# A two-block network: the residual summed on GpSimd and transposed in two parts, the gate weights in one block

## Chip, core and metric

The kernel runs on one core of a Trainium2 chip. The time is the device time of one execution in microseconds (us); three runs are given for the kernel before. TensorE multiplies, VectorE and ScalarE work element by element and read TensorE's results from the banks of PSUM, GpSimd works on SBUF alone, and SyncE (SP) issues the transfers.

## What is computed

512 tokens of 1024 channels go through two blocks. The first is a sliding-window attention beside a gated convolution, and a feed-forward network. The second takes its normalised output `x`, projects it, and mixes it in three ways: a sparse attention with three gated branches, a stick-breaking attention, a gated recurrence. It ends in an output product, a residual and a layer norm. What the change touches is in the second block:

```
h = x @ w_in                                   # among it 18 columns nsa_g
gates = sigmoid(nsa_g)                         # 6 heads x 3 branches
...
mixed = concat(o_nsa * silu(nsa_z), o_sb * silu(sb_z), o_hg * silu(hg_z))
x = layer_norm(ALPHA * x + mixed @ w_out, ln_g, ln_b)
```

and, in the first block, the mask of the sliding window, a constant "band" of 128 x 256.

## The kernel before

Precision is kept by splitting: a weight or an activation `w` becomes a high part `wh` (ScalarE rounds it to fp32r) and a low part `wl = w - wh` (VectorE), and a product is three matmuls: high x high, high x low, low x high. Activations are kept channel-major, 128 channels by 512 tokens; the second block's input is eight pairs `x2[k] = (h, l)` of such tiles.

`dense` (L218) makes one block of 128 output channels: 8 groups of input channels times three matmuls of 512 tokens into one bank. `Weights` loads the blocks ahead through two `raw` tiles, and `split_w` (L189) splits them. `in_proj2` (L800) calls `dense` for each entry of `ORDER`; the fifth, "ng", is the block of the 18 gate columns (L802 gives it 18 output rows), which `gates2` (L728) turns into `gate`: scale, clamp, four small transposes into one bank, Exp, and 1/(1+e). The last eight entries, "z", are the gates of the outputs.

Beside `in_proj2` run the sparse attention (`sparse`, whose `compress`, L857, adds positions to the compressed keys and values on VectorE), the recurrence and `sticks` (the stick-breaking pairs). In `sticks` a pair of heads makes logits, takes a softplus, cuts it to the strict triangle with GpSimd's `affine_select` (L1008; tiles `dk` and `hk`), sums it with the matmuls `pga<-hk,trir`, exponentiates on ScalarE, cuts again (`lv` and `hk`), and multiplies by the values into `poa`. `SEQ` puts the last such pair at the end of that stream.

A planner drives these four tasks by paced costs; the tile framework then orders each engine's instructions by priority and puts in the waits. An engine works strictly in its own order. Banks have five names: "m", "ga", "gb" (two each), "oa", "ob" (one each). A tile or bank that is asked for anew waits until the readers of the one before are done.

At the end stand the output product and the residual. `load_out` (L1239) loads and splits the two halves of `w_out_2`. The residual must be token-major, so all eight `x2` pairs are transposed by plain matmuls against an fp32r identity (`trir[:, 2]`), high and low part into one bank, 64 in all; ScalarE copies the eight banks out, scaled by the token's norm (`rcol`), as `x2t`. Then comes the first half of the product: for each of 8 `mixed` tiles and 4 groups of 128 tokens three matmuls, 96 in all, into four banks. `add` sums product and residual and takes the statistics. The second half goes token group by token group, each with its layer norm and its store.

Of the kernel before, what the change touches and what calls it, by code (L numbers as in the profile page):

```python
# [18 lines left out]
P = 128  # L19
T = 512  # L20
# [19 lines left out]
_off = 0  # L40
for _n, _w in (
    ("ident", 128), ("bones", 128), ("ntri", 128), ("m8", 128),
    ("band", 256), ("valid", 1),
):
    CM[_n] = (_off, _w)
    _off += _w
# [20 lines left out]
def tile_net(ctx, tc, a, out):  # L67
# [114 lines left out]
        return wp.tile([P, 8, P], F32, tag="raw", name=nm("raw"), bufs=2)  # L182

    def fetch(src, nk, w=P):
        raw = raw_tile()[:, :nk, :w]
        nc.sync.dma_start(raw, src)
        return raw

    def split_w(raw, cuts=(0, 8)):  # L189
        nk, w = raw.shape[1], raw.shape[2]  # L190
        wh = wp.tile([P, 8, P], F32R, tag="wh", name=nm("wh"), bufs=2)[:, :nk, :w]
        wl = wp.tile([P, 8, P], F32R, tag="wl", name=nm("wl"), bufs=2)[:, :nk, :w]
        with tc.high_priority(offset=100):
            for c0, c1 in zip(cuts, cuts[1:]):
                c = slice(c0, min(c1, nk))
                A.copy(wh[:, c], raw[:, c])  # L196
                tt(wl[:, c], raw[:, c], wh[:, c].bitcast(F32), ALU.subtract)
        return wh, wl
# [19 lines left out]
    def dense(ws, xs, use, pre=None, tag="m", rows=P, hold=None):  # L218

        ps = bank(tag)[:rows]  # L220
        k, c = 0, 0
        while k < len(xs):
            wh, wl = ws.take()
            for n in range(wh.shape[1]):
                xh, xl = xs[k]
                mm(ps, wh[:, n], xh, k == 0, False)
                mm(ps, wh[:, n], xl, False, False)
                mm(ps, wl[:, n], xh, False, k == len(xs) - 1)
                k += 1
                c += 1  # L230
                if c == 2:
                    c = 0
                    yield 1.3
        if hold is not None and pre is None:
            hold.append((use, ps))
        else:
            if pre:
                pre()
            for u, p in hold or ():
                u(p)  # L240
            use(ps)
        yield 0.65 * c
# [73 lines left out]
    W1.ahead(3, 0)  # L316
    cst = cp.tile([P, CMW], F32, tag="cst", name="cst")
    nc.sync.dma_start(cst, a["const"])

    def S(n, i=0, w=None):  # L320
        o, full = SM[n]
# [135 lines left out]
    def softmax_a(j, ip):  # L457

        ss = [bank(t) for t in ("ga", "gb")]
        lo = [P if ip == 0 and u == 0 else 0 for u in range(2)]  # L460
        for u in range(2):
            i = 2 * ip + u
            for hh in range(2):
                scores(ss[hh][:, u * 256 + lo[u]:u * 256 + 256], qT[j], kv1["k"], hh,
                       slice(i * P, (i + 1) * P), slice((i - 1) * P + lo[u], (i + 1) * P))
        st = small(20)
        sbs = [wk(), wk()]
        for hh in range(2):
            sk = S("sink", j + 4 * hh, 1)
            for u in range(2):  # L470
                c = slice(u * 256 + lo[u], u * 256 + 256)
                n = 2 * hh + u
                V.tensor_tensor_reduce(
                    sbs[hh][:, c], ss[hh][:, c], C("band")[:, lo[u]:], 1.0, sk, ALU.add, ALU.max, st[:, n:n + 1]
                )
        V.tensor_scalar(st[:, 4:8], st[:, 0:4], -1.0, None, ALU.mult)
        for n in range(4):
            hh, u = divmod(n, 2)
            c = slice(u * 256 + lo[u], u * 256 + 256)
            A.activation(sbs[hh][:, c], sbs[hh][:, c], AF.Exp, bias=st[:, 4 + n:5 + n], accum_out=st[:, 8 + n:9 + n])  # L480
        for hh in range(2):
            A.activation(
                st[:, 12 + 2 * hh:14 + 2 * hh], st[:, 4 + 2 * hh:6 + 2 * hh], AF.Exp, bias=S("sink", j + 4 * hh, 1)
            )
        tt(st[:, 8:12], st[:, 8:12], st[:, 12:16], ALU.add)
        V.reciprocal(st[:, 16:20], st[:, 8:12])
        for n in range(4):
            hh, u = divmod(n, 2)
            c = slice(u * 256 + lo[u], u * 256 + 256)
            V.tensor_scalar(sbs[hh][:, c], sbs[hh][:, c], st[:, 16 + n:17 + n], None, ALU.mult)  # L490
        return sbs, lo
# [234 lines left out]
    gate = cp.tile([P, 4, 18], F32, tag="gate", name="gate")  # L726

    def gates2(ps):  # L728
        t = dk()[0:18]
        stt(t, ps, -1.0, rstd3[0:18], ALU.mult, ALU.mult)  # L730
        V.tensor_scalar(t, t, 80.0, None, ALU.min)
        gps = bank("gb")
        for i in range(4):
            TE.transpose(gps[:, 18 * i:18 * i + 18], t[:, i * P:(i + 1) * P], ident[0:18, 0:18])
        A.activation(gate.rearrange("p i h -> p (i h)"), gps[:, 0:72], AF.Exp)
        V.tensor_scalar(gate, gate, 1.0, None, ALU.add)
        V.reciprocal(gate, gate)

        g0 = gate[:, 0].rearrange("p (h b) -> p h b", b=3)[:, :, 0]
        V.tensor_scalar(g0, g0, C("valid"), None, ALU.mult)  # L740
# [59 lines left out]
    def in_proj2():  # L800
        for n, key in enumerate(ORDER):
            yield from dense(W2, x2, use2(key), norm3 if n == 0 else None,  # L802
                             "m" if n > 3 else alt(n), 18 if key == "ng" else P)
            if n == 4:
                token_scale()
        done.add("proj")
# [432 lines left out]
    def load_out(half):  # L1239
        for n, k in enumerate(KORD):  # L1240
            rv = raw_tile()[:, 0:4].rearrange("p a b -> p (a b)")
            nc.sync.dma_start(rv, a["w_out_2"][half, k])
            wo[half, k] = split(rv, None, of("np") if half == 0 else xt if n < 6 else of("hk"))

    load_out(0)


    x2t = [[None] * 2 for _ in range(4)]
    for half in range(2):
        ps = [bank(t) for t in (("ga", "ga", "oa", "ob"), ("m", "m", "gb", "gb"))[half]]  # L1250
        for k in range(4):
            h, l = x2[4 * half + k]
            for i in range(4):
                mm(ps[i][:, k * P:(k + 1) * P], h[:, i * P:(i + 1) * P], trir[:, 2], True, False)
                mm(ps[i][:, k * P:(k + 1) * P], l[:, i * P:(i + 1) * P], trir[:, 2], False, True)
        for i in range(4):
            x2t[i][half] = nk()
            with tc.high_priority(offset=100):
                A.activation(x2t[i][half], ps[i], AF.Copy, scale=rcol[:, i:i + 1])

    load_out(1)
    lng, lnb = (raw_tile().rearrange("p a b -> p (a b)") for _ in range(2))
    nc.sync.dma_start(lng, a["ln_g"].to_broadcast([P, D]))
# [11 lines left out]
    def add(ps, half, i, c=slice(0, T)):  # L1275
# [2 lines left out]
        V.bn_stats(bns[i][:, seen[i]:seen[i] + 6], y)  # L1278
        seen[i] += 6

    po = [bank(t) for t in ("ga", "ga", "oa", "ob")]
    for n in range(KT):
        for i in range(4):
            product(po[i], n, 0, i)
    for i in range(4):
        add(po[i], 0, i)
    for i in range(4):
        for c, t in ((slice(0, T), alt(i)),) if i < 3 else ((slice(0, 256), "ob"), (slice(256, T), "gb")):
            ps = bank(t)[:, 0:c.stop - c.start]
            for n in range(KT):  # L1290
                product(ps, n, 1, i, c)
            add(ps, 1, i, c)
        ag = small(8)
        V.bn_aggr(ag[:, 0:2], bns[i][:, 0:seen[i]])
        A.activation(ag[:, 3:4], ag[:, 1:2], AF.Ln, bias=eps)
        A.activation(ag[:, 3:4], ag[:, 3:4], AF.Exp, scale=-0.5)
        V.tensor_scalar(ag[:, 2:3], ag[:, 1:2], 1e-5 / (ALPHA * ALPHA), None, ALU.add)
        stt(ag[:, 4:5], ag[:, 3:4], ag[:, 2:3], ag[:, 3:4], ALU.mult, ALU.mult)
        V.tensor_scalar(ag[:, 4:5], ag[:, 4:5], -0.5, 1.5, ALU.mult, ALU.add)
        tt(ag[:, 3:4], ag[:, 3:4], ag[:, 4:5], ALU.mult)  # L1300
        for hf in range(2):
            y = x2t[i][hf]
            stt(y, y, ag[:, 0:1], lng[:, T * hf:T * hf + T], ALU.subtract, ALU.mult)
            stt(y, y, ag[:, 3:4], lnb[:, T * hf:T * hf + T], ALU.mult, ALU.add)
            nc.sync.dma_start(out[i * P:(i + 1) * P, T * hf:T * hf + T], y)
# [9 lines left out]
def _constants():  # L1315
# [7 lines left out]
    c["m8"] = (lt & (p[:, None] // 8 != p[None, :] // 8)).astype(f)  # L1323
    k = np.arange(256)
    band = (k[None] > p[:, None]) & (k[None] <= p[:, None] + P)
    c["band"] = np.where(band, 0.0, NEG).astype(f)
    c["valid"] = (p >= 31).astype(f)[:, None]
    const = np.concatenate([c[n] for n in CM], axis=1)
    ms = []
# [7 lines left out]
    oh[b[ok], np.nonzero(ok)[0]] += 1.0  # L1337
    oh[31, ok] -= 1.0
    oh[32, ~ok] = 1.0
    return np.ascontiguousarray(const), cmi, oh  # L1340


def _cols(v):
# [8 lines left out]
def _layout(i):  # L1352
# [6 lines left out]
    for j in range(8):  # L1359
# [12 lines left out]
    rmix = np.concatenate([q2, r(384, 1024)])  # L1372
    f = np.float32
    w_in, w_in2 = i["w_in"][0], i["w_in_2"][0]
    const, cmi, oh = _constants()
    pos = i["cmp_pos_2"][0].reshape(16, 2, 64).transpose(2, 1, 0).reshape(64, 32)
    small = {
        "mix": _cols(i["mix_norm"][0]), "ffn": _cols(i["ffn_norm"][0]), "fin": _cols(i["final_norm"]),
# [10 lines left out]
    return {  # L1389
        "xT": i["x"][0].T.reshape(KT, P, T),  # L1390
        "small": np.concatenate([small[n] for n in SM], axis=1),
        "const": const, "cmask": cmi, "onehot": oh,
        "tbl": np.concatenate([i["rel_bias_2"], np.full((1, 6), NEG, f)], axis=0),
        "w_in": _blocks(w_in[:, cin]),
        "w_br": br,
# [27 lines left out]
```

## Time and profile before

| what | value |
|---|---|
| time, three runs | 1069.88, 1070.99, 1071.37 us (median 1070.99) |
| profiled execution | 1068.53 us, span 1066.8 us |
| TensorE busy | 1039.5 us, 97% of the span, 5712 matmuls |
| VectorE, ScalarE, GpSimd busy | 704.4 (66%), 488.8 (46%), 44.0 us (4%) |
| granted TensorE clock | 0.999 (mean) |
| chain that ended last | TensorE 75%, VectorE 11%, ScalarE 7%, DMA 3% |

The page gives busy times, the chain of waits that ended last, and groups of instructions. Other views of the same execution give busy times by stretch, and the instructions of an engine in order of time. A row there has the start and the length in us, the engine, the line of the kernel, what is written and read, and, in brackets, how long the engine stood idle before it and what ended that. Rows of equal instructions that follow each other are merged ("x4"), and the length is then that of all of them. Matmuls overlap: a start minus the start before is the time that one takes from TensorE, not its length.

### The profile page before, as it was taken

Reading aid. Unit: us, or ns where it says so; the run is one execution under the profiler, and the core shown is the slowest. Engines: PE = TensorE matmul, PEld = TensorE weight load, DVE = VectorE, ACT = ScalarE, POOL = GpSimd, SP = SyncE. Lnnn points to the kernel's source line nnn. Section 1 sums busy time; section 2 is a strip of 40 time slices with the busy share of each in tenths; the row PEclk is TensorE's granted clock in tenths of the full one; section 3 lists DMA queues with packets and bytes.
Section 4 is the critical chain, followed back from the end, with each engine's and each line's share of the span. In section 5 each row is a group of like instructions: output and inputs, shape, how many; then the busy total and the mean of one; then the engine's idle time right before and its main releaser. Section 6 shows DMA issues by size and latency. Waiting matters only on the chain.

```text
span 1066.8 us, 14636 instructions
## 1 busy us (share of the span) xinstructions
PE 1039.5 (97%) x5712; PEld 838.9 (79%) x5712; DVE 704.4 (66%) x1313; ACT 488.8 (46%) x855; POOL 44.0 (4%) x89
## 2 busy tenths in 40 slices
PE   8999999999999999999999999999999999989997
PEld 6788888888888888888877888767777777767886
DVE  6876643356448777777763233597967698887757
ACT  5754443322344444444442222433625676578740
POOL 0000000000220000000000111200000000011000
PEclk9999999999999999999999999999999999999999
DMA  6212232333432233223335333531321110101232
GB/s 218 79 60 80 79 94 85 99 99 109 142 120 85 98 99 99 98 99 99 99 94 193 97 106 90 184 101 41 99 75 47 59 41 22 41 21 37 82 120 79
DMA packets 32801, 97.84 MB, mean 92 GB/s; under 512 B 4878, under 2 KB 5390, under 8 KB 32732
## 3 DMA queue, kind: packets, MB, share of 16 engines
q1 hardware_dynamic: 32732, 96.91, 28.7%
q8 instruction: 45, 0.74, 0.3%
q14 instruction: 24, 0.20, 0.1%
HBM read 94.77 MB, written 5.27 MB: 94 GB/s over the span
## 4 chain that ended last, share of the span: by engine, by line
PE 75%; DVE 11%; ACT 7%; DMA 3%; issue 2%; SPq 1%; POOL 1%; DVEq 0%; POOLq 0%; ACTq 0%
PE pm L139 44%; PE pob L139 12%; PE poa L139 12%; PE pga L139 4%; PE pgb L139 3%; DVE wl L136 2%; DMA raw<-in_w_in 1%; ACT wh L196 1%; DVE lv L136 1%; DMA raw<-in_w_down 1%; DVE hk L136 1%; DVE dk L136 1%; DVE np L136 1%; DVE nk L942 1%; ACT nk L948 1%
## 5 line engine op out<-in xcount | busy, mean ns | idle before, releaser
L139 PE MATMUL pm<-x,wh 128*128 128x512 f32 (+1 forms) x1360 | 433.4, 395 | 2.1 <-DVE x L133 0.9
L139 PEld LDWEIGHTS pm<-x,wh 128*128 128x128 f32 (+1 forms) x1360 | 252.2, 187 | 58.5 <-issue 3.5
L196 ACT CAST wh<-raw 128x1024 fp32r<-128x1024 f32 (+1 forms) x153 | 156.7, 1025 | 275.8 <-issue 109.9
L139 PE MATMUL pm<-x,wl 128*128 128x512 f32 (+1 forms) x680 | 268.3, 395 | 0.0
L136 DVE TENSOR_TENSOR wl<-raw,wh 128x1024 fp32r<-128x1024 f32 (+1 forms) x153 | 181.9, 1189 | 89.5 <-ACT wh L196 87.7
L139 PEld LDWEIGHTS pm<-x,wl 128*128 128x128 f32 (+1 forms) x680 | 127.0, 187 | 26.8 <-issue 1.6
L139 PE MATMUL poa<-x,wh 128*128 128x512 f32 x208 | 65.0, 394 | 0.0
L139 PE MATMUL pob<-x,wh 128*128 128x512 f32 x208 | 64.1, 390 | 0.0
L139 PE MATMUL pm<-np,wh 128*128 128x512 f32 x176 | 54.1, 389 | 0.0
L136 DVE TENSOR_TENSOR dk<-pm,rs 128x512 f32<-128x512 f32 x43 | 29.5, 686 | 28.1 <-PE pm L139 28.0
L139 PEld LDWEIGHTS poa<-x,wh 128*128 128x128 f32 x208 | 39.0, 188 | 9.3 <-issue 1.0
L139 PEld LDWEIGHTS pob<-x,wh 128*128 128x128 f32 x208 | 39.0, 188 | 8.0
L136 DVE TENSOR_TENSOR nk<-pm,rs 128x512 f32<-128x512 f32 x34 | 23.4, 687 | 32.6 <-PE pm L139 32.4
L139 PE MATMUL poa<-x,wl 128*128 128x512 f32 x104 | 40.6, 390 | 0.1
L139 PE MATMUL pob<-x,wl 128*128 128x512 f32 x104 | 40.6, 390 | 0.0
L139 PEld LDWEIGHTS pm<-np,wh 128*128 128x128 f32 x176 | 33.0, 188 | 6.8
L139 PE MATMUL pm<-np,wl 128*128 128x512 f32 x88 | 34.2, 389 | 0.0
L948 ACT ACTIVATE nk<-nk,q 128x128 f32<-128x128 f32 (+3 forms) x48 | 26.5, 555 | 11.5 <-DVE q L946 11.2
L942 DVE CUSTOM_DVE_ANT_0 nk<-pgb,bi 128x128 f32<-128x128 f32 (+3 forms) x48 | 23.1, 484 | 7.9 <-PE pgb L139 7.2
L133 DVE SCALAR_TENSOR_TENSOR dk<-nk,smt,dk 128x511 f32<-128x511 f32 (+1 forms) x34 | 25.4, 748 | 1.4 <-ACT dk L435 0.8
L139 PE MATMUL pgb<-np,np 128*128 128x128 f32 (+3 forms) x96 | 25.9, 351 | 0.4 <-DVE nk L967 0.3
L133 DVE SCALAR_TENSOR_TENSOR nk<-nk,smt,nk 128x511 f32<-128x511 f32 (+2 forms) x33 | 24.7, 747 | 0.5
(498 smaller groups left out, 1664.7 us busy)
## 6 DMA issues: line engine op xcount, KB each, us to landing
raw<-in_w_in SPq DMA_DIRECT2D x65, 512.0 KB, 3.5
raw<-in_w_up SPq DMA_DIRECT2D x44, 512.0 KB, 3.5
raw<-in_w_down SPq DMA_DIRECT2D x16, 512.0 KB, 3.6
raw<-in_w_br SPq DMA_DIRECT2D x8, 512.0 KB, 3.4
raw<-in_w_out SPq DMA_DIRECT2D x8, 512.0 KB, 3.5
raw<-in_w_out SPq DMA_DIRECT2D x16, 256.0 KB, 2.7
raw<-in_w_down SPq DMA_DIRECT2D x8, 384.0 KB, 3.2
d<-d SPq DMA_DIRECT2D x6, 512.0 KB, 6.6
```

The lines of the kernel that those rows point to most:

```text
L133: V.scalar_tensor_tensor(o, i0, s, i1, op0, op1)
L136: V.tensor_tensor(o, i0, i1, op)
L139: return TE.matmul(o, l, r, start=start, stop=stop)
L196: A.copy(wh[:, c], raw[:, c])
L942: V.tensor_tensor_reduce(pb[:, 0:Wd_], s[:, 0:Wd_], bias[h][:, T - Wd_:T], 1.0, -3e38, ALU.add, ALU.max, st[:, g:g + 1])
L948: A.activation(pbs[g][:, 0:Wd_], pbs[g][:, 0:Wd_], AF.Exp, bias=st[:, 2 + g:3 + g], accum_out=st[:, 4 + g:5 + g])
```

## The change

The gates: the block's `raw` tile is filled with zeros behind the 18 columns (GpSimd), the rounded copy covers the whole tile, and the low part is written into columns 32 to 49 of the same tile. One block of weights then holds both parts: `dense` makes two matmuls per group of input channels instead of three, and a product with a constant `sel` (18 columns with two ones each) adds the two rows of results and turns them to token-major. The clamp comes behind that. The "band" leaves the block of constants and is loaded for itself.

The residual: GpSimd adds `h + l` for the eight pairs into tiles `x2f`, of the tags "hk" and "np". Each is transposed as it is (fp32, TensorE's transpose), 16 transposes before the first half of the product and 16 behind it. The banks are named anew.

```diff
 for _n, _w in (
     ("ident", 128), ("bones", 128), ("ntri", 128), ("m8", 128),
-    ("band", 256), ("valid", 1),
+    ("sel", 18), ("valid", 1),
 ):
...
     def fetch(src, nk, w=P):
-        raw = raw_tile()[:, :nk, :w]
-        nc.sync.dma_start(raw, src)
+        raw = raw_tile()[:, :nk]
+        if w < P:
+
+            G.memset(raw[:, :, w:], 0.0)
+            packed.append(raw)
+        nc.sync.dma_start(raw[:, :, 0:w], src)
         return raw
+
+    packed = []
 
     def split_w(raw, cuts=(0, 8)):
         nk, w = raw.shape[1], raw.shape[2]
+        if any(raw is x for x in packed):
+            both = wp.tile([P, 8, P], F32R, tag="wh", name=nm("wh"), bufs=2)
+            with tc.high_priority(offset=100):
+                A.copy(both, raw)
+                tt(both[:, :, 32:50], raw[:, :, 0:18], both[:, :, 0:18].bitcast(F32), ALU.subtract)
+            return both, None
...
                 mm(ps, wh[:, n], xh, k == 0, False)
-                mm(ps, wh[:, n], xl, False, False)
-                mm(ps, wl[:, n], xh, False, k == len(xs) - 1)
+                mm(ps, wh[:, n], xl, False, wl is None and k == len(xs) - 1)
+                if wl is not None:
+                    mm(ps, wl[:, n], xh, False, k == len(xs) - 1)
...
+    band = tl("np")[:, 0:256]
+    nc.sync.dma_start(band, a["band"])
...
-                    sbs[hh][:, c], ss[hh][:, c], C("band")[:, lo[u]:], 1.0, sk, ALU.add, ALU.max, st[:, n:n + 1]
+                    sbs[hh][:, c], ss[hh][:, c], band[:, lo[u]:], 1.0, sk, ALU.add, ALU.max, st[:, n:n + 1]
...
     def gates2(ps):
-        t = dk()[0:18]
-        stt(t, ps, -1.0, rstd3[0:18], ALU.mult, ALU.mult)
-        V.tensor_scalar(t, t, 80.0, None, ALU.min)
+        t = dk()
+        stt(t, ps, -1.0, rstd3, ALU.mult, ALU.mult)
         gps = bank("gb")
         for i in range(4):
-            TE.transpose(gps[:, 18 * i:18 * i + 18], t[:, i * P:(i + 1) * P], ident[0:18, 0:18])
-        A.activation(gate.rearrange("p i h -> p (i h)"), gps[:, 0:72], AF.Exp)
+            mm(gps[:, 18 * i:18 * i + 18], t[:, i * P:(i + 1) * P], C("sel"))
+        flat = gate.rearrange("p i h -> p (i h)")
+        V.tensor_scalar(flat, gps[:, 0:72], 80.0, None, ALU.min)
+        A.activation(flat, flat, AF.Exp)
...
-            wo[half, k] = split(rv, None, of("np") if half == 0 else xt if n < 6 else of("hk"))
+            wo[half, k] = split(rv, None, of("np") if half == 0 else xt)
 
     load_out(0)
 
-
-    x2t = [[None] * 2 for _ in range(4)]
-    for half in range(2):
-        ps = [bank(t) for t in (("ga", "ga", "oa", "ob"), ("m", "m", "gb", "gb"))[half]]
-        for k in range(4):
-            h, l = x2[4 * half + k]
-            for i in range(4):
-                mm(ps[i][:, k * P:(k + 1) * P], h[:, i * P:(i + 1) * P], trir[:, 2], True, False)
-                mm(ps[i][:, k * P:(k + 1) * P], l[:, i * P:(i + 1) * P], trir[:, 2], False, True)
-        for i in range(4):
-            x2t[i][half] = nk()
-            with tc.high_priority(offset=100):
-                A.activation(x2t[i][half], ps[i], AF.Copy, scale=rcol[:, i:i + 1])
-
+    x2f = []
+    for k, (h, l) in enumerate(x2):
+        x2f.append(tl("hk" if k < 4 else "np"))
+        G.tensor_tensor(x2f[k], h.bitcast(F32), l.bitcast(F32), ALU.add)
     load_out(1)
...
+    x2t = [[None] * 2 for _ in range(4)]
+
+    def residual(half, tags):
+        for i in range(4):
+            ps = bank(tags[i])
+            for k in range(4):
+                TE.transpose(ps[:, k * P:(k + 1) * P], x2f[4 * half + k][:, i * P:(i + 1) * P], ident)
+            x2t[i][half] = nk()
+            with tc.high_priority(offset=100):
+                A.activation(x2t[i][half], ps, AF.Copy, scale=rcol[:, i:i + 1])
+
+    residual(0, ("m", "m", "gb", "gb"))
     po = [bank(t) for t in ("ga", "ga", "oa", "ob")]
     for n in range(KT):
         for i in range(4):
             product(po[i], n, 0, i)
     for i in range(4):
         add(po[i], 0, i)
+    residual(1, ("gb", "gb", "m", "m"))
     for i in range(4):
-        for c, t in ((slice(0, T), alt(i)),) if i < 3 else ((slice(0, 256), "ob"), (slice(256, T), "gb")):
+        for c, t in ((slice(0, T), "oa" if i == 2 else "ga"),) if i < 3 else ((slice(0, 256), "ob"), (slice(256, T), "m")):
```

GpSimd, from the last selects of the sticks to the end, before (`hk` is cut on the logits, `lv` and then `hk` on the weights of the last pair):

```order
L1008 AFFINE_SELECT hk_8065<-hk_8065 128x128
L1008 AFFINE_SELECT lv_8067<-lv_8067 128x128
L1008 AFFINE_SELECT lv_8068<-lv_8068 128x128 x2
L1008 AFFINE_SELECT hk_8065<-hk_8065 128x128
L1419 UNCONDITIONAL_BRANCH
```

and after:

```order
L1024 AFFINE_SELECT hk_8059<-hk_8059 128x128
L1266 TENSOR_TENSOR hk_8702<-x_4421,x_4422 128x512
L1266 TENSOR_TENSOR hk_8704<-x_4513,x_4514 128x512
L1266 TENSOR_TENSOR hk_8706<-x_4606,x_4607 128x512
L1266 TENSOR_TENSOR hk_8708<-x_4699,x_4700 128x512
L1024 AFFINE_SELECT lv_8061<-lv_8061 128x128
L1024 AFFINE_SELECT lv_8062<-lv_8062 128x128 x2
L1024 AFFINE_SELECT hk_8059<-hk_8059 128x128
L1266 TENSOR_TENSOR np_8710<-x_4792,x_4793 128x512
L1266 TENSOR_TENSOR np_8712<-x_4885,x_4886 128x512
L1266 TENSOR_TENSOR np_8714<-x_4978,x_4979 128x512
L1266 TENSOR_TENSOR np_8716<-x_5061,x_5062 128x512
```

Four sums stand between the select on the logits and the selects on the weights, four behind them.

TensorE, from the end of the old transposes to the start of the product, before:

```order
L139 MATMUL pm_8753<-trir,x_5060 128x128
L139 MATMUL pgb_8754<-trir,x_5059 128x128
L139 MATMUL pgb_8754<-trir,x_5060 128x128
L139 MATMUL pgb_8755<-trir,x_5059 128x128
L139 MATMUL pgb_8755<-trir,x_5060 128x128
L139 MATMUL pga_8852<-np_8662,lv_8241 128x512
L139 MATMUL pga_8852<-np_8662,lv_8242 128x512
L139 MATMUL pga_8852<-np_8663,lv_8241 128x512
```

and after, from the last transposes into the third bank (`pgb_8788` is `x2t` of token group 2, `pgb_8795` of group 3, `pm_8781` of group 1):

```order
L1294 MATMUL pgb_8788<-cst,hk_8708 128x128
L1294 MATMUL pgb_8795<-cst,hk_8702 128x128
L1294 MATMUL pgb_8795<-cst,hk_8704 128x128
L1294 MATMUL pgb_8795<-cst,hk_8706 128x128
L1294 MATMUL pm_8781<-cst,hk_8702 128x128
L1294 MATMUL pm_8781<-cst,hk_8704 128x128
L1294 MATMUL pm_8781<-cst,hk_8706 128x128
L1294 MATMUL pm_8781<-cst,hk_8708 128x128
L1294 MATMUL pgb_8795<-cst,hk_8708 128x128
L139 MATMUL pga_8802<-np_8656,lv_8235 128x512
```

The transposes of token group 1 stand in the middle of those of group 3, and the product follows directly. The bank of `pm_8781` is that of `pm_8774`, the first four transposes: its first transpose waits for ScalarE's copy of these.

ScalarE at the same place, before (`dk`, `gp` and `bi` belong to the last z blocks, `np` are casts of the product's weights, `rcol` scales the copies of the residual):

```order
L781 ACTIVATE dk_8609<-dk_8609,cc_103 128x512
L783 ACTIVATE dk_8609<-dk_8609 128x512
L250 CAST np_8686<-raw_8684 128x512
L779 ACTIVATE dk_8648<-dk_8646 128x512
L250 CAST np_8692<-raw_8690 128x512
L253 ACTIVATE gp_8617<-dk_8609 128x512
L780 ACTIVATE dk_8648<-dk_8648 128x512
L781 ACTIVATE dk_8648<-dk_8648,cc_103 128x512
L783 ACTIVATE dk_8648<-dk_8648 128x512
L250 CAST np_8698<-raw_8696 128x512
L1259 ACTIVATE nk_8744<-pga_8708,rcol 128x512
L1259 ACTIVATE nk_8746<-pga_8709,rcol 128x512
```

and after:

```order
L799 ACTIVATE dk_8603<-dk_8603 128x512
L263 CAST np_8680<-raw_8678 128x512
L1297 ACTIVATE nk_8779<-pm_8774,rcol 128x512
L795 ACTIVATE dk_8642<-dk_8640 128x512
L1297 ACTIVATE nk_8786<-pm_8781,rcol 128x512
L266 ACTIVATE gp_8611<-dk_8603 128x512
L1297 ACTIVATE nk_8793<-pgb_8788,rcol 128x512
L1297 ACTIVATE nk_8800<-pgb_8795,rcol 128x512
```

The first copy of the residual (`nk_8779<-pm_8774`) stands right behind the cast that follows the last Exp but one of the z blocks; before, the last z block's work and two more casts came in between.

## Rows read from the trace of the kernel before

**Rows 1.** Busy time by stretch: engines (instructions), granted clock, DMA share, GB/s.
```profile
702.60:726.00 23.40, 23.38 (x267) 15.83 (x265) 22.92 (x61) 8.03 (x17) 0.00 (x0) 1.00 0.23 69
...
740.00:940.00 200.00, 194.84 (x1491) 152.57 (x1490) 162.13 (x419) 114.59 (x248) 5.05 (x18) 1.00 0.17 54
940.00:977.20 37.20, 32.32 (x191) 22.84 (x190) 29.93 (x78) 30.38 (x69) 7.04 (x16) 1.00 0.09 29
977.20:1007.30 30.10, 30.10 (x195) 24.84 (x196) 23.05 (x39) 23.50 (x39) 0.00 (x0) 1.00 0.21 62
```

**Rows 2.** TensorE in order of time, gates block: start, length, idle before.
```profile
705.44 0.62 PE L139 MATMUL pm<-x,wh 128*18 128x512 f32 x2
...
706.13 0.62 PE L139 MATMUL pm<-x,wh 128*18 128x512 f32 x2
```

**Rows 3.** TensorE in order of time, residual and output product.
```profile
1007.29 0.56 PE L139 MATMUL pga<-trir,x 128*128 128x128 f32 x4
...
1013.94 0.61 PE L139 MATMUL pgb<-trir,x 128*128 128x128 f32 x4
1015.10 1.66 PE L139 MATMUL pga<-np,lv 128*128 128x512 f32 x6 [0.54 <-ACT nk L1259]
...
1036.99 2.20 PE L139 MATMUL pm<-x,lv 128*128 128x512 f32 x9
```

**Rows 4.** VectorE and TensorE in order of time, behind the gates.
```profile
724.38 2.32 DVE L857 TENSOR_TENSOR nk<-nk,smt 64x248 f32<-64x248 f32 x4
...
726.80 1.97 PE L139 MATMUL pgb<-nk,nk 128*128 128x62 f32 x16 [0.80 <-issue]
...
774.25 0.66 PE L377 MATMUL pgb<-cst,dk 128*128 128x128 f32 x4 [1.51 <-DVE dk L136]
```

**Rows 5.** ScalarE in order of time, beside the residual.
```profile
1008.16 0.60 ACT L250 CAST np<-raw 128x512 fp32r<-128x512 f32 x1
...
1015.52 0.69 ACT L1259 ACTIVATE nk<-poa,rcol 128x512 f32<-128x512 f32 x1
```

**Rows 6.** TensorE in order of time, eight transposes of the attention.
```profile
979.53 1.09 PE L965 MATMUL pgb<-cst,nk 128*128 128x128 f32 x8
980.38 0.70 PE L139 MATMUL pm<-x,wh 128*128 128x512 f32 x2
```

**Rows 7.** GpSimd and TensorE in order of time, last stick-breaking pair.
```profile
970.46 0.62 POOL L1008 TENSOR_SCALAR_AFFINE_SELECT hk<-hk 128x128 f32<-128x128 f32 x1 [5.32 <-DVE hk L133]
975.25 1.65 POOL L1008 TENSOR_SCALAR_AFFINE_SELECT lv<-lv 128x128 f32<-128x128 f32 x3 [4.16 <-ACT lv L1055]
976.85 0.29 POOL L1008 TENSOR_SCALAR_AFFINE_SELECT hk<-hk 128x128 f32<-128x128 f32 x1
...
977.20 1.31 PE L139 MATMUL poa<-lv,gp 128*64 128x128 f32 x20 [0.52 <-POOL hk L1008]
```

**Rows 8.** VectorE and GpSimd in order of time, sums of squares.
```profile
600.80 0.75 DVE L133 SCALAR_TENSOR_TENSOR x<-r,smt,x 128x512 fp32r<-128x512 f32 x1
...
600.91 1.78 POOL L294 TENSOR_TENSOR dk<-dk,nk 128x512 f32<-128x512 f32 x1 [13.18 <-ACT nk L290]
...
678.51 1.26 POOL L294 TENSOR_TENSOR dk<-dk,nk 128x512 f32<-128x512 f32 x1
```

**Rows 9.** VectorE in order of time, last stick-breaking pair.
```profile
970.89 1.27 DVE L136 TENSOR_TENSOR wl<-raw,wh 128x1024 fp32r<-128x1024 f32 x1
972.08 0.41 DVE L136 TENSOR_TENSOR hk<-hk,hk 128x256 fp32r<-128x256 f32 x1
972.61 0.69 DVE L133 SCALAR_TENSOR_TENSOR lv<-dk,lv 128x512 fp32r<-128x512 f32 x1
973.22 0.69 DVE L133 SCALAR_TENSOR_TENSOR dk<-dk,dk 128x512 f32<-128x512 f32 x1
973.83 1.28 DVE L136 TENSOR_TENSOR lv<-lv,pga 128x512 f32<-128x512 f32 x2
975.03 0.68 DVE L136 TENSOR_TENSOR dk<-dk,dk 128x512 f32<-128x512 f32 x1
```

More of the change, by code (lines that the diff above doesn't have):

```diff
@@ L802, in in_proj2 @@
             yield from dense(W2, x2, use2(key), norm3 if n == 0 else None,
-                             "m" if n > 3 else alt(n), 18 if key == "ng" else P)
+                             "m" if n > 3 else alt(n))
             if n == 4:
@@ L1325, in _constants @@
     band = (k[None] > p[:, None]) & (k[None] <= p[:, None] + P)
-    c["band"] = np.where(band, 0.0, NEG).astype(f)
+    c["sel"] = np.zeros((P, 18), f)
+    c["sel"][np.arange(18), np.arange(18)] = 1.0
+    c["sel"][32 + np.arange(18), np.arange(18)] = 1.0
     c["valid"] = (p >= 31).astype(f)[:, None]
@@ L1339, in _constants @@
     oh[32, ~ok] = 1.0
-    return np.ascontiguousarray(const), cmi, oh
+    return np.ascontiguousarray(const), cmi, oh, np.where(band, 0.0, NEG).astype(f)
 def _cols(v):
@@ L1374, in _layout @@
     w_in, w_in2 = i["w_in"][0], i["w_in_2"][0]
-    const, cmi, oh = _constants()
+    const, cmi, oh, band = _constants()
     pos = i["cmp_pos_2"][0].reshape(16, 2, 64).transpose(2, 1, 0).reshape(64, 32)
@@ L1391, in _layout @@
         "small": np.concatenate([small[n] for n in SM], axis=1),
-        "const": const, "cmask": cmi, "onehot": oh,
+        "const": const, "band": band, "cmask": cmi, "onehot": oh,
         "tbl": np.concatenate([i["rel_bias_2"], np.full((1, 6), NEG, f)], axis=0),
```

## The prediction

> **What bounds the kernel now.** I read the busy times by stretch first, then TensorE's waits in order of time, then the two stretches that the change touches, engine by engine. TensorE is busy for 97% of the span. The table by stretch shows how little is left to it where the change lies: 23.38 of 23.40 us while the gates are projected, 194.84 of 200 us after that, all of 30.10 us in the last gate blocks (the z blocks), always at full clock [rows 1]. So a matmul that goes is worth its time, unless the engine that feeds TensorE is as tight. In two places it is. Between 702.6 and 726 us VectorE is busy for 22.92 of 23.40 us. Between 940 and 977.2 us TensorE stands idle for 4.9 us in many small waits, because the second stick-breaking pair runs as one chain through ScalarE, VectorE and GpSimd [rows 1]. The order of the instructions shows that the change puts something into that chain.
>
> **The gates block.** Before, each of the 8 groups of input channels takes three matmuls, 24 in all, with 18 output rows and 512 tokens. Three of them take 706.13 - 705.44 = 0.69 us [rows 2], as the wide ones do: the product's first half makes 96 in 1036.99 - 1015.10 = 21.89 us, 0.228 each [rows 3]. The number of output rows thus costs nothing, and two matmuls per group instead of three remove 8 x 0.23 = 1.8 us of TensorE work. How much comes back? Up to 726 us VectorE is nearly full: it idles 0.48 us [rows 1], and TensorE already waits 0.80 us at 726.80 for the compression's adds, the last of which ends at 724.38 + 2.32 = 726.70 [rows 4] (the profile calls this wait "issue"; the times say VectorE). VectorE's own work shrinks only by the clamp, which moves from 512 to 72 elements. So there at most some 0.7 us can come forward. Behind 726 us VectorE is free again (162.13 of 200 us [rows 1]), and the block after it still has the fewer matmuls in front of it; but at 774.25 TensorE waits 1.51 us for VectorE once more [rows 4], and a TensorE that arrives earlier may only wait longer. The bounds are 0 and 2.6 us (1.8, and the 0.80 too, since the adds are reordered). I take 1.3, between 0.7 and 1.8. At nothing I cost: the memset of the pad (GpSimd has nothing to do there, 0.00 [rows 1], and the load of the weights does not wait for it, only the cast does); the cast over the whole tile (ScalarE is busy for 8.03 of 23.40 us); the low part written into the same tile, as large as before; the four products with the selection matrix in place of four small transposes; the loads of the constants, the band being read only when six blocks of 24 matmuls, 33 us of TensorE, are done. Were the cast's cover gone, it would cost at most 1.4 us, twice the 0.69 that ScalarE takes for 512 elements [rows 5]. On SP's queue the band is one short issue more, ahead of a load that waits for a free tile anyway.
>
> **The residual at the output product.** Before, 64 matmuls against the identity run from 1007.29; 60 of them take 1013.94 - 1007.29 = 6.65 us, 0.111 each. TensorE then waits 0.54 us for a bank, and the second half of the product begins at 1036.99, 29.70 us after the first of the 64 [rows 3]. After, there are 32 transposes of the sum. The kernel has this form elsewhere: 8 in 980.38 - 979.53 = 0.85 us, 0.106 each [rows 6]. 32 x 0.106 = 3.4, and the product's 21.89. But one wait is added: the twelfth of the first 16 transposes goes into the bank of the first four (the order of TensorE below; both are "m" banks and the pool gives the same one out again), so ScalarE must have copied those out. In its order that copy stands behind a cast that runs from 1008.16 to 1008.76 today, and takes 0.69 us [rows 5]: ready at 1009.45, while TensorE is there at 1007.29 + 11 x 0.106 = 1008.46. That is 1.0 us; behind the waiting transposes the whole product is queued. Sum 3.4 + 21.9 + 1.0 = 26.3, against 29.7: 3.4 us gained. Bounds: 4.4 with ScalarE in time, 2.4 with one more cast before the copy. The second 16 transposes stand behind the first half of the product, when their operands are long there. The adds of the first half, which free the banks "ga" for the second half, now have 16 x 0.106 = 1.7 us more. The last split of the second half's weights falls behind the adds on VectorE, but is needed only after 21 of the second half's first 24 matmuls, 4.8 us.
>
> **The eight sums on GpSimd.** They are not in a gap. GpSimd's order has four of them between the last select on the logits (`hk`) and the four selects on the weights of the last stick-breaking pair, the other four behind these. The 40 matmuls of that pair's output wait for the last select, at 977.20 already by 0.52 us [rows 7], and behind them TensorE's queue holds all z blocks, which have no idle time in 30 us [rows 1]. So each microsecond that the selects lose is lost at the end. Before, GpSimd is free from 970.46 + 0.62 = 971.08, and the selects run from 975.25 to 977.14, 1.89 us [rows 7]. How long is an add? Alone 1.26 us at 678.51; 1.78 us at 600.91, where VectorE works on an instruction that reads two operands from SBUF until 601.55: 601.55 + 1.26 = 602.81, and the add ends at 602.69 [rows 8]. So the add waits for such an instruction. Without any wait, four adds end at 971.08 + 5.04 = 976.1, and the selects at 978.0: 0.9 us lost, the lower bound. But VectorE runs such instructions one behind the other from 970.89, and only at 973.83 comes one that reads PSUM [rows 9]. If VectorE goes first each time, the adds run from 973.9 to 978.9, the selects to 980.8: 3.7 us lost. One more instruction of VectorE in between, 0.68 long, makes 4.4. I take 3.9, nearest to these rows. The fourth add is also tied to the last prefix-sum matmul by the slot that it takes over, so it can't come much sooner. The other four adds run beside the z blocks, where VectorE is idle for 30.10 - 23.05 = 7.05 us [rows 1], more than their 4 x 1.26 = 5.0; I cost them at nothing; were half of them exposed, 2.5.
>
> The Trainium skill (SBUF — State Buffer, Who interferes with whom) says that GpSimd and a VectorE instruction with two SBUF inputs hold the read path in turn, each for its whole length, the other blocked. This case's add at 600.91 agrees for GpSimd's side; that VectorE is blocked by an add is shown by no row here. By the rule VectorE's part of the chain moves back too, which is the third rival below.
>
> **Sum.** -1.3 - 3.4 + 3.9 = -0.8 us. The profiled execution took 1068.53 us (span 1066.8 and 1.7 around it), 2.5 below the median of 1070.99; I carry the difference over: 1070.2.
>
> **Rivals.**
> First, faster: the adds do not meet VectorE, or slip into its gaps. For it: the short selects of the same chain lose at most some tenths. Against: the add at 600.91. Then 0.9 stands for 3.9: -1.3 - 3.4 + 0.9 = -3.8, 1067.2.
> Second, the gates return nothing, because VectorE sets the pace of that stretch. For it: 22.92 of 23.40 us, and the waits at 726.80 and 774.25. Against: 200 us of nearly full TensorE behind it. -3.4 + 3.9 = +0.5, 1071.5. That would be the change not doing the half of what it says.
> Third, slower: adds and VectorE take turns between 971 and 981 us. The subtraction at 972.08 and the two instructions behind it each wait for an add, so the operation at 973.83 comes 3 x 1.26 = 3.8 later, with it the prefix-sum matmul and the fourth add, now 1.78 long: 3.8 + 1.8 = 5.6. By the same turns half of the later four adds is exposed, 2.5. 5.6 + 2.5 - 1.3 - 3.4 = +3.4, 1074.4. For it: VectorE's density. Against: the 7.05 us of slack later on. It decides for slower once the adds cost 1.3 + 3.4 + 2.1 = 6.8 us.
>
> **How the numbers follow.** 0.2%, 2.1 us, is about what a measurement of this kernel can tell from no change. The forecast gets 0.45, the first rival 0.25, the second 0.15, the third 0.15. The forecast's own range is 1068.6 to 1071.9 (boundary 1 us either way, gates 0 to 1.8), of which about a fifth is faster by more than 2.1. Faster: 0.24 + 0.09 = 0.33. Slower: 0.13 of the third, 0.01 of the others: 0.14. Same: 0.53. The range leaves out the outer parts of the first and third rival: 1066.3 to 1073.6.
>
> **What would show it.** In the new profile: eight adds of L1266 on GpSimd, the first four between 971 and 980 us (less what the gates give), and a wait of TensorE's `poa` matmuls for GpSimd of some 4 us instead of 0.52; VectorE's wide subtractions there longer than 0.7 us if the third rival is right. The gates block with 16 matmuls, and TensorE at the next wait (774.25 before) earlier by 1.3; if that wait has grown by as much, the gates gave nothing. From the first transposes to the second half of the product 26.3 us in place of 29.7, with about 1 us of waiting for ScalarE. The forecast is wrong if the `poa` wait stays under 2 us or passes 6.

## The result, and the profile after

The changed kernel takes 1076.67 us (median of 4 runs, 1073.43 to 1076.92); the kernel before, beside it, 1070.76. The ratio is 1.0056, with an interval of 1.0042 to 1.007: slower, outside the predicted range. A second set of 6 runs gave 1072.80 us and 1.0037 (1.0025 to 1.005). Of all ten, the four runs at a mean granted clock of 0.988 to 0.990 take 1075.9 to 1076.9 us, the six at 0.993 to 0.996 take 1071.3 to 1073.4. The profiled execution is of the first kind: span 1075.1 us, 8.3 more than that of before.

First the clock, in the table by stretch of the changed kernel. Before, the granted clock was 1.00 in every stretch of [rows 1]; it is half only behind 1063.5 us, when TensorE's last matmul is done (so it is at the end of all twelve profiles, and that end is left out from here on).

```profile
9.40:16.00 6.60, 6.27 (x13) 3.93 (x13) 4.89 (x7) 5.09 (x9) 0.00 (x0) 0.50 0.88 335
16.00:719.40 703.40, 697.60 (x3347) 571.52 (x3345) 426.63 (x657) 284.93 (x432) 31.34 (x43) 1.00 0.33 104
719.40:722.60 3.20, 3.20 (x10) 2.61 (x10) 2.07 (x6) 0.00 (x0) 0.00 (x0) 0.50 0.00 0
...
733.00:736.30 3.30, 3.30 (x13) 2.38 (x14) 1.92 (x4) 0.00 (x0) 0.00 (x0) 0.50 0.00 0
736.30:982.00 245.70, 234.55 (x1759) 180.56 (x1755) 196.10 (x499) 148.08 (x324) 15.55 (x33) 1.00 0.15 48
982.00:988.60 6.60, 5.82 (x30) 4.71 (x32) 5.73 (x10) 4.30 (x8) 4.09 (x6) 0.50 0.00 0
```

Four stretches, 19.7 us together, run at 1.2 GHz instead of 2.4 (0.50 in the column after the five engines). The busy share tells nothing of it: TensorE is "busy" all through them, at half the pace.

Then six instructions that both programs have, in TensorE's order of time (start, length, idle before). Three are from the profile of before:

```profile
25.10 1.12 PE L139 MATMUL pgb<-nk,ones 128*128 128x512 f32 x2
679.83 1.13 PE L139 MATMUL pgb<-dk,ones 128*128 128x512 f32 x2 [0.83 <-POOL dk L294]
785.70 0.66 PE L377 MATMUL pga<-cst,dk 128*128 128x128 f32 x4
```

The other three are in [rows 6] (979.53) and [rows 3] (1007.29, 1036.99). After:

```profile
27.10 1.12 PE L139 MATMUL pgb<-nk,ones 128*128 128x512 f32 x2
682.44 1.13 PE L139 MATMUL pgb<-dk,ones 128*128 128x512 f32 x2 [1.12 <-POOL dk L307]
790.95 0.66 PE L392 MATMUL pga<-cst,dk 128*128 128x128 f32 x4
990.01 1.09 PE L981 MATMUL pgb<-cst,nk 128*128 128x128 f32 x8
1019.41 0.60 PE L1294 MATMUL pm<-cst,hk 128*128 128x128 f32 x4
1045.03 2.33 PE L139 MATMUL pga<-x,lv 128*128 128x512 f32 x9
```

The differences are 2.00, 2.61, 5.25, 10.48, 12.12 and 8.04 us. So the account by stage, beside the prediction's (0.3 us more of the 8.3 lie behind the last row):

| stretch | profile | forecast |
|---|---|---|
| start (half clock from 9.40) | +2.0 | 0 |
| up to the sums of squares | +0.6 | 0 |
| gates and compression | +2.6 | -1.3 |
| last stick-breaking pair | +5.2 | +3.9 |
| z blocks | +1.6 | 0 |
| residual and first half of the product | -4.1 | -3.4 |

In the pair, what happened stands on VectorE; it answers to [rows 9]:

```profile
976.08 1.26 DVE L136 TENSOR_TENSOR wl<-raw,wh 128x1024 fp32r<-128x1024 f32 x1
977.26 1.51 DVE L136 TENSOR_TENSOR hk<-hk,hk 128x256 fp32r<-128x256 f32 x1
978.70 1.77 DVE L133 SCALAR_TENSOR_TENSOR lv<-dk,lv 128x512 fp32r<-128x512 f32 x1
980.39 1.75 DVE L133 SCALAR_TENSOR_TENSOR dk<-dk,dk 128x512 f32<-128x512 f32 x1
982.06 1.27 DVE L136 TENSOR_TENSOR lv<-lv,pga 128x512 f32<-128x512 f32 x2
```

The subtraction grows from 0.41 to 1.51, the next two from 0.69 to 1.77 and 1.75: 3.24 us more, some 1.08 for each. Beside them GpSimd, which answers to [rows 7]:

```profile
975.64 0.62 POOL L1024 TENSOR_SCALAR_AFFINE_SELECT hk<-hk 128x128 f32<-128x128 f32 x1 [5.32 <-DVE hk L133]
976.24 5.35 POOL L1266 TENSOR_TENSOR hk<-x,x 128x512 f32<-128x512 f32 x3
...
983.66 1.40 POOL L1266 TENSOR_TENSOR hk<-x,x 128x512 f32<-128x512 f32 x1 [2.08 <-PE pga L139]
985.03 1.24 POOL L1024 TENSOR_SCALAR_AFFINE_SELECT lv<-lv 128x128 f32<-128x128 f32 x3
```

Three sums run between 976.24 and 981.59, and each of the three VectorE instructions waits for one of them. The instruction behind, with one operand in PSUM, has its old length but starts at 982.06. TensorE waits for it, then runs at half clock until 988.6:

```profile
978.83 1.13 PE L139 MATMUL pga<-hk,trir 128*128 128x256 f32 x8 [0.43 <-DVE hk L136]
...
982.78 1.12 PE L139 MATMUL pga<-hk,trir 128*128 128x256 f32 x4 [2.31 <-DVE lv L136]
...
986.56 2.40 PE L139 MATMUL poa<-lv,gp 128*64 128x128 f32 x20
```

### The profile page after: what moved, and what is told of

It reads as the page before. It is cut to its first block, busy times and chain, and to the rows that moved or that the text cites. A ratio compares the mean times of both kernels' runs of the same rounds, so it can differ in the third digit from the quotient of the medians.

```text
span 1075.1 us, 14582 instructions
## 1 busy us (share of the span) xinstructions
PE 1043.7 (97%) x5676; PEld 842.9 (78%) x5676; DVE 711.7 (66%) x1313; ACT 489.1 (45%) x855; POOL 57.5 (5%) x98
## 4 chain that ended last, share of the span: by engine, by line
PE 76%; DVE 12%; ACT 7%; issue 3%; DMA 1%; POOL 1%; SPq 0%; DVEq 0%; POOLq 0%; ACTq 0%
PE pm L139 43%; PE poa L139 13%; PE pob L139 12%; PE pga L139 4%; PE pgb L139 3%; DVE wl L136 2%; DVE hk L136 1%; DVE dk L136 1%; DVE lv L136 1%; ACT wh L208 1%; DVE dk L133 1%; DVE nk L958 1%; DVE np L136 1%; DVE nk L971 1%; ACT nk L964 1%
## 5 line engine op out<-in xcount | busy, mean ns | idle before, releaser
L139 PE MATMUL pm<-x,wh 128*128 128x512 f32 x1360 | 436.0, 398 | 2.1 <-ACT x L266 1.1
L139 PEld LDWEIGHTS pm<-x,wh 128*128 128x128 f32 x1360 | 255.7, 190 | 57.7 <-issue 3.2
L139 PE MATMUL pm<-x,wl 128*128 128x512 f32 x672 | 267.5, 398 | 0.0
L139 PEld LDWEIGHTS pm<-x,wl 128*128 128x128 f32 x672 | 127.5, 190 | 26.9 <-issue 1.6
```

The source lines that it names most:

```text
L139: return TE.matmul(o, l, r, start=start, stop=stop)
```

## The experiments

The measured ratios are all against the kernel before, run beside them, which takes 1069.2 to 1069.4 us there (79 runs).

**Each half of the change alone.** The kernel before with the gates and band edits of the diff, nothing else:

> The gates and band edits alone, the residual as before. Theory A (the gates edit itself costs, by the eight small selection products, by the compression adds that come later on VectorE and by two stretches at half clock behind them): the profile of the changed kernel lies 3.2 us later over this stretch, so about 1074 us against 1070.8, and TensorE's clock falls to half between 715 and 740 us again. Rival B (the half clock there is a matter of chance, the edit returns its 1.3 us): about 1069.5 us and full clock.

Measured: 1069.41 us, ratio 1.0001 (0.9987 to 1.0014). Neither: the edit is worth nothing, as the prediction's second rival had it. The interval, -1.4 to +1.5 us, does not by itself leave out a gain of 1.3; that the two other pairs of old and new gates below (0.9964 and 0.9966, 1.0031 and 1.0037) show none either speaks against it. Its profile has one stretch at half clock (727 to 732 us); the mean clock of its runs is 0.992 to 0.997, that of the kernel before 0.992 to 0.999.

The kernel before with the residual edit alone (GpSimd sums, 32 transposes in two parts, the banks, the second half's weights in "x" tiles):

> The residual edit alone, gates and band as before. Theory A (GpSimd's sums and VectorE's operations with two SBUF operands take turns, the last stick-breaking pair and the z blocks lose 5.3 + 1.6 us, the boundary at the output product gains 3.8): about 1070.8 + 3.1 = 1073.9 us; the three VectorE operations behind the split of the weights last 1.5 to 1.8 us in place of 0.41 and 0.69. Rival B (the loss comes with the half clock and the later arrival of the gates stage): 1067.4 to 1069 us.

Measured: 1072.8 us, ratio 1.0031 (1.0021 to 1.004). Theory A holds in time and in rows; the three VectorE instructions last 1.51, 1.77 and 1.75 us here too. In TensorE's order of time, against 977.20 [rows 7] and 979.53 [rows 6] of before:

```profile
977.35 0.68 PE L139 MATMUL pga<-hk,trir 128*128 128x256 f32 x4 [2.31 <-DVE lv L136]
...
981.12 2.40 PE L139 MATMUL poa<-lv,gp 128*64 128x128 f32 x20 [0.62 <-POOL hk L1008]
...
985.30 1.09 PE L965 MATMUL pgb<-cst,nk 128*128 128x128 f32 x8
```

The `poa` matmuls start 3.9 us late, and 0.3 more since this execution came 0.3 early to the pair (its sums of squares at 679.55 against 679.83): 4.2. They then run at half clock, as the clock column shows (0.50), and the next transposes are 5.8 late, 1.9 more.

```profile
0.00:978.50 978.50, 957.58 (x5234) 768.96 (x5235) 645.50 (x1199) 446.88 (x780) 48.01 (x89) 1.00 0.27 92
978.50:985.00 6.50, 5.88 (x43) 4.87 (x44) 3.81 (x6) 3.13 (x7) 3.81 (x6) 0.50 0.00 0
```

**The changed kernel without the sums.**

```diff
-        x2f.append(tl("hk" if k < 4 else "np"))
-        G.tensor_tensor(x2f[k], h.bitcast(F32), l.bitcast(F32), ALU.add)
+        x2f.append(h.bitcast(F32))
```

> The changed kernel without the eight GpSimd sums: the transposes read the high parts directly, so the low parts of the residual are left out. Theory A (the sums cost 5.3 us in the last pair and 1.6 in the z blocks, with the half clock that follows the wait): 1076.7 - 6.9 = 1069.8 us, VectorE's operations there 0.41 and 0.69 us again, no half clock behind 970 us. Rival B (the stall of the pair is carried on from the gates stage): no better than 1075 us.

Measured: 1065.44 us, ratio 0.9972 (0.9958 to 0.9986): faster than the kernel before. The three VectorE instructions last 0.41, 0.69 and 0.69 us again, and the clock is full from the start to 1057 us. The gates' late arrival did not make the stall. Theory A had the time too high, since it started from the first set's 1076.7; from the second set's 1072.8 the same 6.9 us give 1065.9.

**The sums behind the last select.**

```diff
+        tc.add_manual_dep(i.ins, picked[0], ...)   # the last select of the last pair
```

> The changed kernel with the eight GpSimd sums tied behind the last select of the last stick-breaking pair, so that all eight run beside the z blocks. Theory A (turns with VectorE wherever they meet): the pair's 5.3 us come back, but eight sums stretch VectorE's operations in the z blocks, at least twice the 1.4 us of waits that four of them made: 1076.7 - 5.3 + 1.4 to 2.8, 1072.8 to 1074.2 us. Rival B (only the selects behind the sums mattered, the z blocks have VectorE to spare): 1070 us.

Measured: 1069.74 us, ratio 1.0007 (0.9994 to 1.002). From the second set's 1072.8, theory A's terms give 1068.9 to 1070.3. Rival B's 1070 lies in that range, so the time does not decide; the trace bears out theory A: the `poa` wait is 0.52 us as before, and TensorE waits in the z blocks instead, 1.03 + 0.37 + 1.04 us. From the eight transposes to the residual's first it is 1011.29 - 980.46 = 30.8 us, 3.1 more than before, about twice the 1.6 of the changed kernel:

```profile
989.74 0.63 PE L981 MATMUL pgb<-cst,nk 128*128 128x128 f32 x4 [1.03 <-DVE nk L971]
990.74 0.63 PE L981 MATMUL pgb<-cst,nk 128*128 128x128 f32 x4 [0.37 <-DVE nk L971]
...
993.33 1.10 PE L139 MATMUL pob<-nk,np 128*64 128x128 f32 x16 [1.04 <-DVE nk L983]
```

**The changed kernel again.**

> The changed kernel itself, beside the same runs of the kernel before as the next ones. Theory A (the two halves of the change add up: 0.1 us for the gates alone, 3.3 to 3.6 for the residual alone): 1.0032 times the kernel before, about 1072.7 us where that takes 1069.2. Rival B (the two together cost more, as the first four runs had it, since each brings its own stretches at half clock): 1.0056 times, 1075.2 us.

Measured: 1072.8 us, 1.0037. The interval takes in 1.0032 and its end lies below 1.0056: the halves add up, and most of the surplus of the first set belonged to runs at a low clock.

**The sums on VectorE**, four behind the last select, four behind the first 16 transposes:

```diff
-        G.tensor_tensor(x2f[k], h.bitcast(F32), l.bitcast(F32), ALU.add)
+        i = V.tensor_tensor(x2f[k], h.bitcast(F32), l.bitcast(F32), ALU.add)
+        tc.add_manual_dep(i.ins, picked[0], ...)   # last select; for k > 3 the copy of the first transposes
```

> The changed kernel with the eight sums on VectorE: four behind the last select, four behind the first transposes. Theory A (only the meeting of GpSimd with VectorE was dear; VectorE has 7 us to spare beside the z blocks and half of its time beside the product, and a sum takes 0.69 us): as without any sums, a factor of 0.997 to 0.998 on the kernel before, 1066 to 1067 us. Rival B (the four sums lie in the way of the z blocks' chain on VectorE and show as waits of TensorE, 4 x 0.69 = 2.8 us): 1068.2 us or more.

Measured: 1065.29 us, ratio 0.9966 (0.9953 to 0.9978), as without any sums. Eight sums cost nothing measurable on VectorE and 7 us on GpSimd. The run moves the sums to another engine and to another place at once. The z blocks tell the two apart: with four sums of VectorE in front of and beside them it is 1011.66 - 790.07 = 221.59 us from the transposes at 790.07 (785.70 before) to the residual's first, to the hundredth as before (1007.29 - 785.70); the four sums of GpSimd beside them cost 1.6 us. So there it is the meeting that is dear, not the work. What four sums of VectorE would cost in front of the selects, no run shows.

**The gates' tail ahead of the compression's adds.**

```diff
+        with tc.high_priority(offset=2000):
             V.tensor_scalar(flat, gps[:, 0:72], 80.0, None, ALU.min)
             A.activation(flat, flat, AF.Exp)
             V.tensor_scalar(gate, gate, 1.0, None, ALU.add)
             V.reciprocal(gate, gate)
```

> The gates edit alone, with the clamp, the exponential, the sum and the reciprocal of the gates given a high priority, so that they come ahead of the compression's adds as in the kernel before and not between them. Theory A (the gates return nothing because their late tail lies between the adds that TensorE waits for, 0.32 + 1.32 us in place of 0.80): the waits fall to 0.8 us or less, and 0.8 to 1.2 us come back: 1068.0 to 1068.4 us where the kernel before takes 1069.2. Rival B (VectorE's total work sets the pace up to the wait in front of the next gate block, whatever its order): no change, 1069.2 us, with the wait near 774 us grown by what the compression gains.

Measured: 1070.85 us, ratio 1.0018 (1.0006 to 1.003). Theory A falls. The tail is out of the way, yet TensorE waits longer (1.33 us for 0.80). Counted from the sums of squares (679.15 us here, 679.83 before) the row comes after 47.49 us, with the gates alone after 47.44 (726.19 - 678.75), before after 46.97 [rows 4].

```profile
726.64 2.00 PE L139 MATMUL pgb<-nk,nk 128*128 128x62 f32 x16 [1.33 <-DVE nk L874]
```

So up to this row the order does not matter, as rival B says. Its other sign did not come: the wait near 774 us shrank, to 1.00 us. Nor did its time: 1070.85 is 1.6 us above the kernel before. The trace does not show why, since it is of the fastest of the 12 runs (1067.91). The same in the changed kernel with both edits:

> The whole change with the sums on VectorE as in the kernel of that name and the tail of the gates ahead of the compression's adds. If both theories A hold: 3.0 us for the residual and 1.0 for the gates, 1065.2 us where the kernel before takes 1069.2. If only the first holds: 1066.2 us. If neither: 1068 us or more.

Measured: 1066.18 us, ratio 0.9971 (0.9959 to 0.9983): the time of the first theory alone. The interval, 1064.9 to 1067.4 us, takes in that of both too; against the second theory stands the run before.

**Is it the wait that lowers the clock?** Ten matmuls in front of the one that waits 2.31 us:

```diff
+    for _ in range(10):
+        f = mm(po, x2[0][0][:, 0:P], x2[0][0], True, True)
```

> The residual edit alone, with ten more matmuls of 512 columns (10 x 0.227 = 2.3 us, into the bank of the attention's output before that is written) in front of the prefix-sum matmul that waits 2.31 us for VectorE. They do nothing for the result. Theory A (TensorE's clock falls to half because it stands idle there; the 6.1 us at half clock cost some 1.7 us by the offsets of the trace, 3 by their length): the wait is gone, the clock stays full between 974 and 990 us, and the kernel takes 1.7 to 3 us less than without them, 1069.8 to 1071.1 where the kernel before takes 1069.2 (without them 1072.5 to 1072.8). Rival B (the half clock has nothing to do with that wait, and 2.3 us of more matmuls only fill it): 1072.5 us or a little more, the half clock stays.

Measured: 1071.83 us, ratio 1.0025 (1.0016 to 1.0034), against 1.0031 without them: between the theories, and not told apart by the time. The ten matmuls also moved the fourth sum on GpSimd to between the selects, and the wait with it:

```profile
976.83 2.50 PE L139 MATMUL poa<-x 128*128 128x512 f32 x10
979.86 0.68 PE L139 MATMUL pga<-hk,trir 128*128 128x256 f32 x4 [0.53 <-DVE lv L136]
...
984.68 1.75 PE L139 MATMUL poa<-lv,gp 128*64 128x128 f32 x20 [2.26 <-POOL hk L1008]
```

The table by stretch of the same kernel shows full clock where the wait was filled, and half behind the new one:

```profile
976.80:979.40 2.60, 2.53 (x12) 1.78 (x11) 2.60 (x3) 0.16 (x1) 1.86 (x2) 1.00 0.13 52
979.40:985.30 5.90, 3.18 (x24) 2.51 (x26) 4.73 (x10) 5.20 (x11) 4.01 (x6) 1.00 0.00 0
985.30:988.60 3.30, 3.30 (x35) 2.97 (x32) 2.61 (x5) 1.33 (x4) 0.57 (x1) 0.52 0.00 0
```

The half clock went with the wait, which speaks for theory A's cause; its price stays open.

**The best: sums on VectorE, old gates.**

> The residual edit alone with the sums on VectorE, the gates and the band as in the kernel before; the same with the new gates took a factor of 0.9966 on the kernel before. Theory A (the gates edit returns nothing either way): 0.996 to 0.9975, 1065.0 to 1066.5 us. Rival B (the gates edit saves 1 us of work but lowers the clock by as much and more): below 0.996. Rival C (the gates edit is worth its 1 us, the run of it alone hid that by chance): 0.9975 or more, 1066.5 us.

Measured: 1064.63 us, ratio 0.9964 (0.9952 to 0.9977), the same as with the new gates (0.9966). Theory A: the gates edit is worth nothing. This kernel beats both, the one before by 0.36%, with a span of 1062.7 us. Two of its first four sums stand in VectorE's gap before the z blocks, the other two between instructions that keep their length, and the pair waits 0.50 us as before:

```profile
977.98 0.68 DVE L1257 TENSOR_TENSOR hk<-x,x 128x512 f32<-128x512 f32 x1
...
981.57 0.68 DVE L1257 TENSOR_TENSOR hk<-x,x 128x512 f32<-128x512 f32 x1
```

```profile
977.30 1.31 PE L139 MATMUL poa<-lv,gp 128*64 128x128 f32 x20 [0.50 <-POOL hk L1008]
```

## Why the prediction was wrong

**The sums on GpSimd are the step that failed.** The prediction took 3.9 us for them; they cost 1.0031 - 0.9964 = 0.0067 of 1069.4, 7.2 us. Three parts were missing or mis-sized.

- Who waits. The step said "if VectorE goes first each time". The rows show turns: each VectorE instruction waits for the sum that is under way, and each sum for the instruction. That is the third rival, to the instruction (three, at 976 to 982 us); it was given 0.15. Its 3 x 1.26 = 3.8 us measured 3.24, its 5.6 for the whole pair 4.2. The rule that stood beside it, in the Trainium skill (SBUF — State Buffer, Who interferes with whom), says that the second to issue is blocked until the first ends; this trace agrees, 0.41 us becoming 1.51. The `poa` matmuls came 4.2 us late in the run of the residual alone, so the forecast's 3.9 was near by luck, by the wrong mechanism: TensorE's long wait is for VectorE, at the prefix sums (2.31 us). At `poa` it waits 0.62 us there and not at all in the changed kernel, under the 2 us that the prediction named as the sign of being wrong.
- The clock. The prediction read "always at full clock" in the profile of before and carried it over. Behind the 2.31 us wait the clock is halved for 6.5 us, 1.9 us more in the run of the residual alone; the prediction had no term for it. It is so in all three profiles with that wait (the changed kernel twice, the residual alone) and in none of the eight without it (before, the gates alone, without sums, sums late, tail first, the three with sums on VectorE).
- The later four sums, costed at nothing, since VectorE had 7.05 us to spare. The slack would have held the work, as the run with the sums on VectorE shows. But on GpSimd they stretch VectorE's instructions on the way to TensorE, which waits 0.38 + 1.03 us for them; the z blocks lose 1.6 us. The stages of the residual alone (4.2 and 1.9 in the pair, 1014.76 - 985.30 = 29.46 in place of 27.76 in the z blocks) add up to 7.8, near the 7.2 of the runs.

```profile
998.88 0.63 PE L981 MATMUL pgb<-cst,nk 128*128 128x128 f32 x4 [0.38 <-DVE nk L971]
...
1001.47 1.09 PE L139 MATMUL pob<-nk,np 128*64 128x128 f32 x16 [1.03 <-DVE nk L983]
```

**The gates were mis-sized too**: about 0.1 us in place of -1.3; the second rival had the number. Three things ate it. The products with the selection matrix, costed at nothing, take 1.07 us; the transposes they replace took 0.42, and the instruction behind them started 716.46 - 716.19 = 0.27 us after them, now 718.57 - 717.58 = 0.99. Of before:

```profile
716.19 0.42 PE L734 MATMUL pgb<-cst,dk 18*128 18x18 f32 x4
716.46 1.03 PE L139 MATMUL pgb<-ones,rs 1*128 1x2 f32 x8
```

After (the last two rows answer to the 0.80 us of [rows 4]):

```profile
717.58 1.07 PE L139 MATMUL pgb<-cst,dk 128*128 128x18 f32 x8
718.57 1.29 PE L139 MATMUL pgb<-ones,rs 1*128 1x2 f32 x8
...
728.92 1.16 PE L139 MATMUL pga<-lv 64*128 64x128 f32 x16 [0.31 <-DVE hk L1190]
731.41 2.36 PE L139 MATMUL pgb<-nk,nk 128*128 128x62 f32 x16 [1.32 <-DVE nk L873]
```

What is left meets the compression's adds, where TensorE waits 0.31 + 1.32 us in place of 0.80 [rows 4]. The value should have been near the lower end of the bounds (0 to 2.6), where VectorE's 22.92 of 23.40 us [rows 1] pointed.

The third is the clock. In the run without the sums, which has the new gates and full clock here, the stage takes 784.76 - 679.33 = 105.43 us:

```profile
679.33 1.12 PE L139 MATMUL pgb<-dk,ones 128*128 128x512 f32 x2 [0.77 <-POOL dk L307]
784.76 0.66 PE L392 MATMUL pga<-cst,dk 128*128 128x128 f32 x4
```

Before it took 785.70 - 679.83 = 105.87, so the edit brought 0.4 us. With the gates alone it took 785.76 - 678.75 = 107.01: 1.1 us lost, with some 4 us at half clock right behind the 1.32 us wait. Such a stretch stands there in five of the eight profiles with the new gates and in none of the four with the old ones. How much of the missing gain each of the three took in a usual execution, the runs don't tell.

**The residual at the output product was right, and a little small**: 1019.41 to 1045.03 is 25.6 us, forecast 26.3. The wait for ScalarE came, at 0.17 us here and 0.52 in the run of the residual alone, in place of 1.0:

```profile
1020.95 0.66 PE L1294 MATMUL pm<-cst,hk 128*128 128x128 f32 x4 [0.17 <-ACT nk L1297]
1021.47 1.63 PE L139 MATMUL pga<-np,lv 128*128 128x512 f32 x6
```

With the sums off GpSimd the whole residual edit is worth 1 - 0.9964, 3.9 us.

**The sum, once more.** 0.1 - 3.9 + 7.2 = +3.4 us by the runs of the two halves alone, against -0.8; the second set of the changed kernel measured +3.6. The two rivals that came true add up to 5.6 + 2.5 - 3.4 = +4.7, which was nowhere in the list, since each rival changed one term. What stays open is the rest of the first set's +5.9. Three of its four runs had a clock of 0.990 or less, and the half clock at the start of the profiled one (2.0 us) begins in front of the first instruction that the change adds (the band's load, issued at 11.28 us); what makes the clock fall in one execution and not in the next, the runs don't tell.

## What to carry to other kernels

An elementwise operation that is moved to an idle GpSimd is not free while VectorE works on SBUF operands: look for the VectorE instructions beside it, and count each as waiting for one whole operation, on the way to whoever waits for VectorE. VectorE's idle time over a stretch hid the sums that it made itself, not those of GpSimd; ask which instructions are stretched and who waits for them. And where a forecast adds a wait of TensorE, ask what it costs if the clock falls behind it: here it fell behind each wait of 2.3 us, and behind some of 1.3.

## What was not expected of the hardware

- A GpSimd sum also holds up a VectorE operation with one tensor operand: `nk<-nk,q` (L971, 128x512) took 1.50 us beside the later sums, 0.48 elsewhere.

```profile
995.14 0.48 DVE L971 TENSOR_SCALAR nk<-nk,q 128x512 f32<-128x512 f32 x1
995.54 1.77 DVE L136 TENSOR_TENSOR dk<-dk,r 128x512 f32<-128x512 f32 x1
997.24 1.50 DVE L971 TENSOR_SCALAR nk<-nk,q 128x512 f32<-128x512 f32 x1
```

- Granted clock and time go together from run to run of one kernel: of 79 runs of the kernel before, 25 at 0.998 and 0.999 average 1068.6 us, 14 at 0.997 average 1069.1, 36 at 0.995 and 0.996 average 1069.7, and 4 at 0.992 to 0.994 average 1073.0. Its single executions so differ by more than this change is worth.
- The clock also fell without a wait to speak of: at 719.4 us of the changed kernel TensorE had been busy since 716.20, with 0.18 us of idle time ahead of that, on the small matmuls of the compression, the selection and the `ones` rows shown above. And it does not fall behind every wait: the one near 774 us, 1.51 to 1.53 us long in the four profiles with the old gates, is followed by full clock in all four.
